# The recurrence's gate products: one 128-row block-diagonal product per gate, or two 64-row tiles of TensorE that each carry both gates of one block

## The chip, the cores and the metric

The kernel runs on one core of a Trainium2 chip. The metric is the device time of one launch in microseconds (us), the median over several runs. One further execution was recorded by the hardware profiler; it gives the rows that are read below.

## The reference, cut to what matters

The model is a two-layer hybrid backbone on 512 latent tokens and 256 context tokens of width 1024. Each layer mixes tokens with four branches (retention, latent attention, a gated linear recurrence called RG-LRU, and a state-space branch), merges them by gates, projects, and then runs a convolutional feed-forward part. The change touches the gates of the recurrence alone. Its 512 channels are 8 blocks of 64; each block has a 64 x 64 weight for each of two gates and two scan directions:

```python
def gates(u, d):
    ub = u.reshape(b, t, LRU_BLOCKS, LRU_BLOCK).astype(f32)
    z = einsum('btnc,gncd->gbtnd', ub, gate_w[d]).reshape(2, b, t, w) + gate_b[d]
    r, i = sigmoid(z[0]), sigmoid(z[1])
    log_a = -LRU_C * r * softplus(-lam[d])
    return exp(log_a), sqrt(-expm1(2.0 * log_a)) * (i * u)
```

The two results feed a scan over the tokens, forward for d = 0 and backward for d = 1.

## The kernel before

Activations lie channel by channel: a feature tile holds 128 channels on the 128 partitions and 768 tokens (256 of context, 512 latent) along the columns. Every float32 product is done as three single-pass products of a value's rounded high part and its low rest (high x high, high x low, low x high), which accumulate in one PSUM bank. A weight unit is a 128 x 1024 array: a DMA on the queue of the sync engine (SP) brings it into a raw buffer (`wr`, 3 buffers), ScalarE (ACT) rounds it into `wh` (L205, 5 buffers), and VectorE (DVE) forms `wl` in two halves (L143, 5 buffers).

The recurrence (`lru`) goes over four feature tiles f, and for each of them over the two directions d. `project(f)` makes the convolved input `u` and an output gate; `scan(f, d)` makes the gates and runs the scan. A feature tile holds two blocks of 64 channels, and the host lays their 64 x 64 weights into a 128 x 128 matrix whose other two quarters are zero; one weight unit holds eight such matrices (two feature tiles, two directions, two gates). In `scan`, for each gate and each of the two token segments (256 and 512 columns), one bank `z` of the four-bank pool `c` takes three products with K = 128 rows and 128 output columns of the array, and one ACT instruction (L1057, tanh with the gate's bias from `gb`) writes it to SBUF. `gb` is half of the gate's bias, by channel, made once a layer in `layer_prep`.

A scheduler sets each engine's order from priorities and dependences. Between the pieces of `lru` it places the work of the queued merges (`merge`: the sigmoid gate and the branch's projection of the branch that was finished before, products into the four banks of pool `g`, read by ACT at L1325), and parts of the modulation weights for later (`ada_all`, L317: four products of 32 output columns side by side on TensorE). After `lru`, the merge of its own results follows, and then the output projection.

Of the kernel before, what the change touches and what calls it, by code (L numbers as in the profile page):

```python
# [8 lines left out]
F32 = mybir.dt.float32  # L9
# [7 lines left out]
P = 128  # L17
# [17 lines left out]
# buffers: 256-column and 512-column scratch, raw weights, their low and high parts, split columns  # L35
MEM = (4, 4, 3, 5, 5, 4)
N_T, N_O, N_WR, N_WL, N_WH, N_V = MEM
# slots of 768 columns in the token mixer; in the feed-forward, and of 512 columns
N_SLOT = 27
# weight of the queued merge work placed behind each piece of a branch  # L40
# [11 lines left out]
# up-projections of latent tokens begun before the last pair of the post norm, by layer  # L52
N_EARLY = (6, 6)
# units of the output projection that go unsplit, in float32 products, for a layer and a token pair
PLAIN = {(0, 0): (0, 1, 2, 3, 4, 5, 6, 7), (1, 2): (3, 5, 7)}
# last units of a product held back so that the output banks finish one after another: output projection, down-projection, its last pair; by layer
STAG = ((0, 2), (0, 0), (3, 5))
# both tiles of a pair normalised before either is scaled, by the same places
PW = ((1, 1), (0, 0), (1, 1))
# order of the pieces of retention: c, d: the two parts of a head; q, k, v, g: projections; y: merges  # L60
RORD = [('c', 0), ('q',), ('d', 0), ('g', 2), ('c', 1), ('k',), ('d', 1), ('v',), ('c', 2), ('g', 3), ('d', 2), ('c', 3), ('y',), ('d', 3), ('y',)]
# query tiles by which transposes and values trail the attention weights; heads by which the sums within chunks trail their matrices
# [5 lines left out]
# buffers that modulation weights take: raw, high, low  # L68
ADA_R = 'hlhl'
ADA_T = ("rhlr", "hlrh", "lrhl", "hlhl")  # L70
# first token pairs loaded behind the first two blocks of modulation weights
FP = {0: (1, 2), 1: (0,)}
# priorities: transposes behind post norms, weights, post norms, split columns, merges
# [6 lines left out]
# offsets of the shape-only tables in the constant array  # L80
# [8 lines left out]
# offsets of the per-partition vectors of a layer  # L89
# [9 lines left out]
def trunk(tc, xin, cc, const, pv, pr, rows, ada_b, ada_w, w_in, w_uq, w_ukv, w_lg, w_br, w_out, w_up, w_dn, out):  # L99
# [9 lines left out]
    with ExitStack() as ctx:  # L109
# [64 lines left out]
        def load_tables(names):  # L174
            """tables that a layer needs for a while."""
# [48 lines left out]
        def fm(wh, wl, nk, x, segs):  # L224
            """feature-major product: weights [128, nk, 128] against x[k] = (hi, lo) over token segments."""
            res = []
            for off, n in segs:
                ps = G()
                for k in range(nk):
                    xh, xl = x[k]  # L230
                    mm3(ps[:, 0:n], wh[:, k, :], wl[:, k, :], xh[:, off:off + n], xl[:, off:off + n], k == 0, k == nk - 1)
                res.append((ps, off, n))
            return res

        def tm(units, cols, x, pairs, begun=None, nk_all=None):
            """token-major product: units = list of ((hi, lo), nk), x[k] = (hi, lo); one bank per token pair; begun: (banks, k) of its first part."""
# [19 lines left out]
        def log1p_of(o, u, n):  # L256
            """o = log1p(u) for u in [0, 1], as 2 atanh(u / (2 + u))."""
# [25 lines left out]
        def ada_part(l, b, tags):  # L283
            """512 columns of a layer's modulation of both streams, four parts over the contraction side by side on TensorE."""
# [10 lines left out]
        def ada_col(l, b, src, n):  # L295
            """bias and place of a vector's blocks b to b + n, by columns: src [128, s, 4 n]"""
# [4 lines left out]
        def ada_store(l, b, r):  # L301
            """the parts' sums"""
# [5 lines left out]
        def ada_all(groups):  # L308
            """four blocks side by side on TensorE."""
# [35 lines left out]
        def ln_stats(halves, eps=LN_EPS):  # L345
            """mean and 1/std of a token tile given as column pieces."""
# [10 lines left out]
        def to_hT(l, which, pair, xh, hT, kps=(0, 1, 2, 3)):  # L357
            """transpose normalised token tiles of a pair, modulate, split."""
# [33 lines left out]
        def load_gate(l, which, s):  # L392
            """a stream's gate spread over the partitions."""
# [6 lines left out]
        def load_bc(l, which):  # L400
            """the norm's weight and bias spread over the partitions, and the latent gate."""
# [8 lines left out]
        def load_res(pair, res):  # L410
            """the residual of a pair of token tiles."""
# [7 lines left out]
        def post_norm(pair, ps, rs, bc, dst, again, wait=False):  # L419
            """new residuals of a token pair from its products ps[a][half]; normalised once more for the next product."""  # L420
# [41 lines left out]
        def pair_of(t, p, spare=False):  # L462
            """the split columns of a pair of token tiles; spare: into the space of a layer's normalised input."""
# [15 lines left out]
        def tm_wide(units, nk, xsl, last=0):  # L479
            """one pair of token tiles against [128, 1024] units, contraction outermost but for the last units."""  # L480
# [37 lines left out]
        # =====================================================================  # L518
        def layer_prep(l):
# [11 lines left out]
            # log(sigmoid(decay)) and softplus(-lambda)  # L531
# [16 lines left out]
            gb = lp.tile([P, 16], F32, tag="gb", name=nm("gb"))  # L548
            ts(gb, V("lgb"), 0.5, MUL)
            q["gb"] = gb  # L550
            q["lg"] = lg
            # halved coefficients
# [12 lines left out]
            # ssd  # L565
# [9 lines left out]
        def retention(q, W, hT, full, outs, begun=None):  # L575
# [6 lines left out]
            def project(dst, h, pairs, begun=None):  # L582
                """a quantity of heads h and h + 1, token-major."""
# [11 lines left out]
            def rope(x3):  # L595
                """on the latent tokens"""
# [9 lines left out]
            def queries(h):  # L606
                """of heads h and h + 1, feature-major; the halves that the rotation mixes are brought together by DMA"""
# [20 lines left out]
            def core(h):  # L628
# [4 lines left out]
                # transposes  # L633
# [15 lines left out]
                # states  # L649
# [18 lines left out]
                # within chunks and outputs  # L668
# [69 lines left out]
            # retention decays  # L738
# [963 lines left out]
```

## Time and profile before

| | us |
|---|---|
| median of 3 runs | 2877.71 |
| lowest and highest run | 2874.56, 2879.39 |
| profiled execution, first to last instruction (span) | 2876.2 |
| TensorE (PE) busy in it | 2824.4 |
| ScalarE (ACT) busy | 1244.0 |
| VectorE (DVE) busy | 1861.2 |

The profiled execution lists no time around its span, and the span lies inside the range of the runs. A matmul's listed duration (0.28 us for 256 columns, 0.39 to 0.40 us for 512) runs from its start to the end of its last result, and the next one starts before that end; what a matmul costs in a full stream is the distance from its start to the next start. `PEld` is the loading of weights into the array, which runs beside the matmuls.

### The profile page before, as it was taken

What the parts mean: (1) busy time and instruction counts of PE and PEld (TensorE: products, weight loads), DVE (VectorE), ACT (ScalarE), POOL (GpSimd) and SP (SyncE); (2) the same over time, 40 slices, a digit from 0 to 9 for tenths busy, and PEclk for the clock granted to TensorE, in tenths of its full rate; (3) what the DMA queues carried; (4) which work ended last, traced back from release to release, by engine and by line L of the source; (5) the groups of instructions that cost most, each with busy time, mean ns of one, the idle gap of its engine ahead of it and who ended that gap; (6) DMA issues with size and microseconds to landing.
All of it is one profiled execution on the core that took longest, in us unless ns stands there. A gap on an engine that the chain in (4) does not pass through costs nothing.

```text
span 2876.2 us, 41735 instructions
## 1 busy us (share of the span) xinstructions
PE 2824.4 (98%) x16136; PEld 2409.4 (84%) x16136; DVE 1861.2 (65%) x3885; ACT 1244.0 (43%) x2190; POOL 53.2 (2%) x70
## 2 busy tenths in 40 slices
PE   7999999999999999999999999999999999899998
PEld 5999878888888886888888779988888888688887
DVE  6463347767566448755557876545887685886667
ACT  4323235434456334533335653244444573453353
POOL 0000000000000001000000000000000000000000
PEclk9999999999999999999999999999999999999999
DMA  7212450445353346422226663122034334543365
GB/s 264 73 42 89 164 176 16 151 165 189 118 169 118 105 153 191 131 61 65 66 88 193 192 196 112 51 90 81 24 103 142 103 118 141 200 148 101 95 197 177
DMA packets 117591, 363.75 MB, mean 126 GB/s; under 512 B 13793, under 2 KB 14177, under 8 KB 117393
## 3 DMA queue, kind: packets, MB, share of 16 engines
q1 hardware_dynamic: 117392, 361.08, 39.0%
q8 instruction: 127, 2.08, 0.3%
q14 instruction: 72, 0.58, 0.1%
HBM read 332.59 MB, written 26.35 MB: 125 GB/s over the span
## 4 chain that ended last, share of the span: by engine, by line
PE 84%; DVE 8%; DMA 4%; ACT 2%; issue 1%; POOL 1%; SPq 0%; POOLq 0%; DVEq 0%; ACTq 0%
PE g L220 18%; PE g L221 17%; PE g L222 17%; PE g L250 4%; PE g L251 4%; PE g L252 4%; PE g L486 3%; PE g L489 3%; PE g L490 2%; DVE wl L143 2%; PE g L946 1%; DVE o L143 1%; DMA wr<-in_w_dn_dram 1%; PE g L317 1%; DVE st L349 1%
## 5 line engine op out<-in xcount | busy, mean ns | idle before, releaser
L143 DVE TENSOR_TENSOR wl<-wr,wh 128x512 fp32r<-128x512 f32 x866 | 566.8, 682 | 459.8 <-ACT wh L205 458.8
L220 PE MATMUL g<-hh,wh 128*128 128x512 f32 (+1 forms) x2384 | 841.8, 353 | 0.8 <-ACT s L510 0.7
L221 PE MATMUL g<-hl,wh 128*128 128x512 f32 (+1 forms) x2384 | 837.7, 351 | 0.0
L222 PE MATMUL g<-hh,wl 128*128 128x512 f32 (+1 forms) x2384 | 837.5, 351 | 0.0
L205 ACT CAST wh<-wr 128x1024 fp32r<-128x1024 f32 (+1 forms) x433 | 451.6, 1045 | 642.8 <-PE g L221 325.1
L220 PEld LDWEIGHTS g<-hh,wh 128*128 128x128 f32 x2384 | 451.1, 189 | 66.5 <-issue 5.9
L222 PEld LDWEIGHTS g<-hh,wl 128*128 128x128 f32 x2384 | 450.8, 189 | 58.3
L221 PEld LDWEIGHTS g<-hl,wh 128*128 128x128 f32 x2384 | 451.2, 189 | 57.1
L251 PE MATMUL g<-wh,hl 128*128 128x256 f32 (+1 forms) x816 | 231.3, 284 | 1.7 <-DVE hl L143 1.7
L250 PE MATMUL g<-wh,hh 128*128 128x256 f32 (+1 forms) x816 | 232.1, 285 | 0.1
L252 PE MATMUL g<-wl,hh 128*128 128x256 f32 (+1 forms) x816 | 231.8, 284 | 0.0
L143 DVE TENSOR_TENSOR s<-s,s 128x256 f32<-128x256 f32 (+4 forms) x332 | 206.7, 645 | 34.7 <-ACT s L1065 14.7
L486 PE MATMUL g<-wh,t 128*128 128x512 f32 x468 | 185.0, 397 | 3.5 <-ACT t L216 2.5
L489 PE MATMUL g<-wh,t 128*128 128x512 f32 x468 | 184.6, 396 | 1.4 <-DVE t L143 1.1
L490 PE MATMUL g<-wl,t 128*128 128x512 f32 x468 | 183.5, 395 | 1.0 <-DVE wl L143 0.6
L221 PE MATMUL g<-s,wh 128*128 128x512 f32 (+1 forms) x452 | 160.6, 355 | 0.0
L220 PE MATMUL g<-s,wh 128*128 128x512 f32 (+1 forms) x452 | 160.2, 354 | 0.0
L222 PE MATMUL g<-s,wl 128*128 128x512 f32 (+1 forms) x452 | 159.9, 354 | 0.0
L251 PEld LDWEIGHTS g<-wh,hl 128*128 128x128 f32 x816 | 156.5, 192 | 2.3 <-DVE hl L143 2.1
L250 PEld LDWEIGHTS g<-wh,hh 128*128 128x128 f32 x816 | 156.7, 192 | 1.5 <-issue 0.8
L252 PEld LDWEIGHTS g<-wl,hh 128*128 128x128 f32 x816 | 156.5, 192 | 0.2
L152 DVE SCALAR_TENSOR_TENSOR s<-g,pv,s 128x511 f32<-128x511 f32 (+2 forms) x176 | 111.7, 643 | 61.2 <-ACT s L510 59.3
(284 smaller groups left out, 4107.3 us busy)
## 6 DMA issues: line engine op xcount, KB each, us to landing
wr<-in_w_in_dram SPq DMA_DIRECT2D x144, 512.0 KB, 3.6
wr<-in_w_dn_dram SPq DMA_DIRECT2D x110, 512.0 KB, 4.4
wr<-in_w_up_dram SPq DMA_DIRECT2D x100, 512.0 KB, 3.7
wh<-in_ada_w_dram SPq DMA_DIRECT2D x46, 512.0 KB, 3.6
wl<-in_ada_w_dram SPq DMA_DIRECT2D x46, 512.0 KB, 4.6
wr<-in_w_out_dram SPq DMA_DIRECT2D x40, 512.0 KB, 4.1
wr<-in_w_br_dram SPq DMA_DIRECT2D x32, 512.0 KB, 3.6
acc<-s SPq DMA_DIRECT2D x24, 384.0 KB, 3.3
```

The lines of the kernel that those rows point to most:

```text
L143: dve.tensor_tensor(out=o, in0=a, in1=b, op=op)
L152: dve.scalar_tensor_tensor(out=o, in0=a, scalar=s, in1=b, op0=op0, op1=op1)
L205: act.copy(hi[:, 0:f], raw[:, 0:f])
L220: pe.matmul(o, lhsT=sh, rhs=mh, start=start, stop=False)
L221: pe.matmul(o, lhsT=sh, rhs=ml, start=False, stop=False)
L222: pe.matmul(o, lhsT=sl, rhs=mh, start=False, stop=stop)
L250: pe.matmul(o, lhsT=sh, rhs=wkh, start=first, stop=False, skip_group_check=True)
L251: pe.matmul(o, lhsT=sl, rhs=wkh, start=False, stop=False, skip_group_check=True)
L252: pe.matmul(o, lhsT=sh, rhs=wkl, start=False, stop=last, skip_group_check=True)
L486: pe.matmul(ps[a][h], lhsT=xh, rhs=wh[:, cs], start=k == 0, stop=wl is None and k == nk - 1)
L489: pe.matmul(ps[a][h], lhsT=xl, rhs=wh[:, cs], start=False, stop=False)
L490: pe.matmul(ps[a][h], lhsT=xh, rhs=wl[:, cs], start=False, stop=k == nk - 1)
```

## The change

Three things change, all for the gates of the recurrence.

1. The weights. Of each 128 x 128 block-diagonal matrix only the two 64 x 64 quarters that aren't zero are fetched (`blocks`): two DMAs of 64 partitions, each with eight pieces of 64 values (256 bytes) a partition, pack them into 512 columns of the raw buffer. Rounding and low part are made of 512 columns in one ACT and one DVE instruction.
2. The products. For a direction, the two gates' 64 columns of one block now stand beside each other, so 64 rows x 128 columns hold both gates of one block. A product of block 0 uses rows 0 to 63 of TensorE and writes bank `z[0]`; the product of block 1 uses rows 64 to 127 and writes `z[1]`. For each segment these come in pairs, for the three parts of the split. Products in all: 12 a scan as before, each with half the rows.
3. The evictions. A bank now holds gate 0 in its upper and gate 1 in its lower 64 partitions, of one block of channels. Each needs its own target, so a bank is read by two ACT instructions on 64 partitions each: 8 a scan, where there were 4. Where source and target lie in different halves, the bias must too: `gb` gets 16 more columns with the halves exchanged, by two DMAs of 64 x 16 values and one more DVE instruction a layer.

The diff's core (the rest removes comments):

```diff
-            gb = lp.tile([P, 16], F32, tag="gb", name=nm("gb"))
-            ts(gb, V("lgb"), 0.5, MUL)
+            gb = lp.tile([P, 32], F32, tag="gb", name=nm("gb"))
+            o = _PO["lgb"][0]
+            for a, b in ((0, 64), (64, 0)):
+                sy.dma_start(out=gb[a:a + 64, 16:32], in_=pv[l][b:b + 64, o:o + 16])
+            ts(gb[:, 0:16], V("lgb"), 0.5, MUL)
+            ts(gb[:, 16:32], gb[:, 16:32], 0.5, MUL)
...
+            def blocks(ap):
+                with tc.high_priority(offset=O_UNIT):
+                    raw, hi, lo = W4("wr", N_WR, F32), W4("wh", N_WH), W4("wl", N_WL)
+                    src = ap.rearrange("p (m b c) -> p m b c", m=8, b=2)
+                    for b in range(2):
+                        r = slice(64 * b, 64 * b + 64)
+                        sy.dma_start(out=raw[r, 0:512].rearrange("p (m c) -> p m c", m=8), in_=src[r, :, b, :])
+                    split(raw[:, 0:512], hi[:, 0:512], lo[:, 0:512])
+                return hi, lo
...
-                        gm[0] = unit(WG(f // 2), shape=(8, 128))
+                        gm[0] = blocks(WG(f // 2))
...
-                for g, dst in ((0, t0), (1, t1)):
-                    i = 4 * (f % 2) + 2 * d + g
-                    j = 8 * d + 4 * g + f
-                    for off, n in (SEG_C, SEG_L):
-                        z = C()
-                        mm3(z[:, 0:n], gm[0][0][:, i, :], gm[0][1][:, i, :], gm[1][0][:, off:off + n], gm[1][1][:, off:off + n], True, True)
-                        act.activation(out=dst[:, off:off + n], in_=z[:, 0:n], func=AF.Tanh, scale=0.5, bias=q["gb"][:, j:j + 1])
+                i = 4 * (f % 2) + 2 * d
+                for off, n in (SEG_C, SEG_L):
+                    z = [C(), C()]
+                    for p, (w, x) in enumerate(((0, 0), (0, 1), (1, 0))):
+                        for b in range(2):
+                            r = slice(64 * b, 64 * b + 64)
+                            pe.matmul(z[b][:, 0:n], lhsT=gm[0][w][r, 64 * i:64 * i + 128], rhs=gm[1][x][r, off:off + n], start=p == 0, stop=p == 2)
+                    for b in range(2):
+                        for g, dst in ((0, t0), (1, t1)):
+                            j = 8 * d + 4 * g + f + (0 if g == b else 16)
+                            r = slice(64 * g, 64 * g + 64)
+                            act.activation(out=dst[64 * b:64 * b + 64, off:off + n], in_=z[b][r, 0:n], func=AF.Tanh, scale=0.5, bias=q["gb"][r, j:j + 1])
```

How the order moves, first on TensorE, at the products of layer 0's first scan (f = 0, d = 0) behind their first part; `c_` are the banks, `s_7966` and `s_7967` the high and low part of `u`, `wh_` and `wl_` the gate weights. Before:

```order
L222 MATMUL g_8010<-hh_104,wl_8007 128x512
L221 MATMUL c_7973<-s_7967,wh_7961 128x256
L222 MATMUL c_7973<-s_7966,wl_7963 128x256
L221 MATMUL c_7978<-s_7967,wh_7961 128x512
L222 MATMUL c_7978<-s_7966,wl_7963 128x512
L221 MATMUL c_7983<-s_7967,wh_7961 128x256
L222 MATMUL c_7983<-s_7966,wl_7963 128x256
L221 MATMUL c_7988<-s_7967,wh_7961 128x512
L222 MATMUL c_7988<-s_7966,wl_7963 128x512
L220 MATMUL g_8010<-hh_106,wh_8005 128x512
```

The same place now, with `s_7969` and `s_7970` for the two parts of `u`:

```order
L222 MATMUL g_8017<-hh_104,wl_8014 128x512
L1074 MATMUL c_7976<-s_7970,wh_7963 128x256
L1074 MATMUL c_7977<-s_7970,wh_7963 128x256
L1074 MATMUL c_7976<-s_7969,wl_7964 128x256
L1074 MATMUL c_7977<-s_7969,wl_7964 128x256
L1074 MATMUL c_7988<-s_7970,wh_7963 128x512
L1074 MATMUL c_7989<-s_7970,wh_7963 128x512
L1074 MATMUL c_7988<-s_7969,wl_7964 128x512
L1074 MATMUL c_7989<-s_7969,wl_7964 128x512
L220 MATMUL g_8017<-hh_106,wh_8012 128x512
```

The products stand in the same place among the merge's (`g_`), and the same number of them; two that follow each other now go to different banks, and belong to different halves of the array's rows. Over the whole program the 192 products stand in 24 unbroken runs among other products: runs of 4 and 8 in a scan of d = 0, and of 12 in one of d = 1.

Second on ACT, the evictions of the same scan and what follows them. Before:

```order
L1057 ACTIVATE s_7970<-c_7973,gb_579 128x256
L1057 ACTIVATE s_7970<-c_7978,gb_579 128x512
L1057 ACTIVATE s_7971<-c_7983,gb_579 128x256
L1057 ACTIVATE s_7971<-c_7988,gb_579 128x512
L1060 ACTIVATE s_7972<-s_7970,l_576 128x768
```

Now:

```order
L1079 ACTIVATE s_7973<-c_7976,gb_579 64x256
L1079 ACTIVATE s_7974<-c_7976,gb_579 64x256
L1079 ACTIVATE s_7973<-c_7977,gb_579 64x256
L1079 ACTIVATE s_7974<-c_7977,gb_579 64x256
L1079 ACTIVATE s_7973<-c_7988,gb_579 64x512
L1079 ACTIVATE s_7974<-c_7988,gb_579 64x512
L1079 ACTIVATE s_7973<-c_7989,gb_579 64x512
L1079 ACTIVATE s_7974<-c_7989,gb_579 64x512
L1082 ACTIVATE s_7975<-s_7973,l_576 128x768
```

Eight instructions on 64 partitions stand where four on 128 stood, ahead of the same chain of exponential and square root.

Third on SP's queue, at the start of the program, where `pv` and `pr` are layer 0's small vectors and the `wr_` are the first weight units of retention. Before:

```order
L522 DMA pv_539<-in_pv_dram 128x277
L524 DMA pr_541<-in_pr_dram 128x48
L198 DMA wr_697<-in_w_in_dram 128x1024
L198 DMA wr_763<-in_w_in_dram 128x1024
L333 DMA o_3782<-in_ada_b_dram 32x512
```

Now:

```order
L522 DMA pv_539<-in_pv_dram 128x277
L524 DMA pr_541<-in_pr_dram 128x48
L552 DMA gb_579<-in_pv_dram 64x16 x2
L198 DMA wr_700<-in_w_in_dram 128x1024
L198 DMA wr_766<-in_w_in_dram 128x1024
```

The two small DMAs of `gb` stand ahead of two weight units; on ACT, DVE and TensorE the work of the next 20 us is then ordered a little differently. Outside of this place, of the two recurrences and of what is woven with them, the engines' orders are as they were, but for layer 1's two `gb` DMAs and its DVE instruction, which now stand behind layer 0's recurrence.

## Rows read from the trace of the kernel before

**Rows 1.** The page's head, and its first part: busy us, share of span, instructions.
```profile
span 2876.2 us, 41735 instructions
PE 2824.4 (98%) x16136; PEld 2409.4 (84%) x16136; DVE 1861.2 (65%) x3885; ACT 1244.0 (43%) x2190; POOL 53.2 (2%) x70
```

**Rows 2.** Both recurrences by stretch: window, length, busy PE, PEld, DVE, ACT, POOL, clock.
```profile
775.00:945.00 170.00, 169.95 (x985) 143.00 (x984) 116.01 (x154) 104.31 (x135) 0.00 (x0) 1.00 0.41 137
...
2195.00:2385.00 190.00, 190.00 (x923) 159.67 (x922) 139.77 (x209) 120.85 (x164) 1.01 (x1) 1.00 0.41 130
```

**Rows 3.** The chain that ended last, within 775 to 945 us: shares by line.
```profile
by line: PE g L220 28.2%; PE g L221 28.1%; PE g L222 28.0%; PE g L317 4.4%; PE c L220 4.0%; PE c L222 3.5%; PE c L221 3.4%; PE c L326 0.5%; issue 0.0%
```

**Rows 4.** Line L222's third products: ns min/median/max, first and last start, forms.
```profile
L222 PE MATMUL c<-s,wl x64: 274/337/497, 779.5 to 2369.6; 128*128 128x256 f32 x32, 128*128 128x512 f32 x32
```

**Rows 5.** PE in order of time, one whole scan (start us, us, operation).
```profile
2264.44 0.28 PE L220 MATMUL c<-s,wh 128*128 128x256 f32 x1
2264.55 0.28 PE L221 MATMUL c<-s,wh 128*128 128x256 f32 x1
...
2266.31 0.39 PE L222 MATMUL c<-s,wl 128*128 128x512 f32 x1
2266.54 0.39 PE L220 MATMUL g<-hh,wh 128*128 128x512 f32 x1
```

**Rows 6.** PE in order of time, round 16 side-by-side products of 32 columns.
```profile
790.52 0.40 PE L221 MATMUL c<-s,wh 128*128 128x512 f32 x1
790.84 0.62 PE L317 MATMUL g<-wh,silu 128*32 128x512 f32 x1
...
791.30 0.59 PE L317 MATMUL g<-wh,silu 128*32 128x512 f32 x1
...
792.16 0.59 PE L317 MATMUL g<-wh,silu 128*32 128x512 f32 x1
...
792.70 0.50 PE L222 MATMUL c<-s,wl 128*128 128x512 f32 x1
793.03 0.28 PE L220 MATMUL c<-s,wh 128*128 128x256 f32 x1
```

**Rows 7.** Weight loads (PEld) in order of time at the same place.
```profile
790.84 0.11 PEld L317 LDWEIGHTS g<-wh,silu 128*32 128x32 f32 x1 [0.36 <-issue]
...
790.89 0.11 PEld L317 LDWEIGHTS g<-wl,silu 128*32 128x32 f32 x1
```

**Rows 8.** PE in order of time: products of 64 columns, each with a 128-column load.
```profile
2117.87 1.00 PE L1244 MATMUL c<-s,s 128*128 128x64 f32 x8
2118.68 0.36 PE L221 MATMUL g<-hl,wh 128*128 128x256 f32 x1
```

**Rows 9.** Groups of ACT instructions by form (count, busy us, mean ns).
```profile
L1057 ACT ACTIVATE s<-c,gb 128x512 f32<-128x512 f32 x32 | 22.2, 693 | 1.0 <-PE c L222 1.0
L1057 ACT ACTIVATE s<-c,gb 128x256 f32<-128x256 f32 x32 | 15.1, 473 | 5.5 <-PE c L222 5.5
L1136 ACT COPY s<-c 16x384 f32<-16x384 f32 x4 | 1.6, 457 | 0.0
```

**Rows 10.** ACT in order of time: a first scan's evictions.
```profile
2258.92 2.10 ACT L1057 ACTIVATE s<-c,gb 128x256 f32<-128x256 f32 x4 [0.82 <-PE c L222]
```

**Rows 11.** DMA issues by line: engine, count, KB each, median us to landing.
```profile
wr<-in_w_lg_dram SPq DMA_DIRECT2D x4, 512.0 KB, 4.3
```

**Rows 12.** SP's queue in order of time: second gate unit of layer 0.
```profile
832.11 0.57 SPq L198 DMA_DIRECT2D wr<-in_w_lg_dram  x1
```

**Rows 13.** PE in order of time: first products with that unit.
```profile
863.50 0.97 PE L220 MATMUL c<-s,wh 128*128 128x256 f32 x4
```

**Rows 14.** DVE in order of time, at the first use of the small vectors.
```profile
37.40 0.17 DVE L534 COPY z<-pv 128x8 f32<-128x8 f32 x1 [0.38 <-DMA pv<-in_pv_dram]
...
45.48 0.17 DVE L147 TENSOR_SCALAR s<-z 128x16 f32<-128x16 f32 x1
```

**Rows 15.** SP's queue in order of time: weight units issued behind the small vectors.
```profile
29.55 11.73 SPq L198 DMA_DIRECT2D wr<-in_w_in_dram  x2
```

## The prediction

> **What bounds the kernel now.** I read the page's first part first, since the share of each engine says where to look: TensorE is busy for 2824.4 of 2876.2 us [rows 1], so what isn't on TensorE hardly shows in the total. Shares are means, so the second view is the busy time of the two stretches that hold the recurrences: PE 169.95 of 170.00 us and 190.00 of 190.00, ACT 104 and 121, DVE 116 and 140, at the granted clock's higher level, 2.4 GHz (the 1.00 in the row) [rows 2]. The third is the chain of waits in the first of them: it consists of PE's matmuls, with no share of ACT, DVE or DMA, and the gate products are the lines "PE c" [rows 3]. So a microsecond taken from PE there is a microsecond of the total, as long as ACT and DVE still deliver; and an operation added to ACT costs nothing until it makes PE wait.
>
> **The change part by part.**
>
> The products. The third products of the gates are 64, half of 256 and half of 512 columns [rows 4]; three products a gate and segment make 192. In a stream, a product of 256 columns costs 0.12 us to the next start, one of 512 costs 0.23, and the twelve of a scan together 2266.54 - 2264.44 = 2.10 us [rows 5]. Sixteen scans (4 tiles, 2 directions, 2 layers) make 33.6 us. Now there are 96 pairs, and if the two of a pair run side by side, a pair costs what one costs: 48 x (0.23 + 0.12) = 16.8 us, so 16.8 us go. The trace has no product of 64 rows. The nearest rows are the products of 32 columns, four side by side: sixteen of them, in four groups, pass between 790.84 and 792.70, and a group takes (792.16 - 791.30) / 2 = 0.43 us, for four products at once [rows 6]. So this chip does run tiles of the array at the same time, by columns. The two bounds are 16.8 us saved and 0 saved (the pairs follow each other as before). I take 16.8, by the row of the side-by-side products.
>
> The loads of weights. Each product loads its own 128 columns of weights. Where the stream is short, the load sets the pace: eight products of 64 columns take 2118.68 - 2117.87 = 0.81 us, 0.10 each [rows 8]. A pair needs two loads, 0.20 us if they follow each other: hidden behind a pair of 512 columns (0.23), not behind one of 256 (0.12). With four column tiles the loads don't follow each other: eight of 32 columns begin between 790.84 and 790.89, each 0.11 long [rows 7], though eight quarters of 0.10 would be 0.20 us one behind the other. I take it that loads into different tiles overlap, and keep the other as a rival.
>
> The changes of tiling. Round the side-by-side products the trace shows a price: 790.52 to 790.84 is 0.32 where a product of 512 costs 0.23 (+0.09), the first group 0.46 instead of 0.43 (+0.03), the last 0.54 (+0.11), and the first product behind it 0.33 instead of 0.23 (+0.10) [rows 6]. That is 0.33 us for a way in and out. The order has 24 runs of paired products among products that use the whole array, so 24 x 0.33 = 7.9 us come back. Bounds: nothing, if a switch to half the rows costs less than one to a quarter of the columns; and, if each side waits for the last result (0.40 - 0.23 = 0.17 us beyond a product's place [rows 5, 6]) and then for a load of 0.11 [rows 7], 0.28 a switch, 24 x 0.56 = 13.4 us. I take 7.9. "TensorEngine Tiling (Array Packing)", section "Key Properties", in the Trainium skill, says that a change of the tiling mode drains TensorE, which a change of tile alone does not. The trace agrees in kind, by the 0.33 us; the rule speaks for keeping the paired products in few long runs, and here runs of 4 and 8 stand where one of 12 could.
>
> The evictions. Four instructions on 128 partitions, 0.473 and 0.693 us by form, become eight on 64. By these rows an eviction of 16 partitions and 384 columns takes 0.457 us [rows 9], so time goes by columns and I charge the eight in full: 4.2 us instead of 2.10 [rows 10], 16 x 2.1 = 34 us more on ACT (at least 0, if half the partitions took half the time). What hides it: ACT has 66 of 170 and 69 of 190 us free [rows 2]. Behind the evictions on ACT stand the exponentials of the same scan and a weight unit's rounding; the one who could wait on PE is the next scan's first product, which needs the four banks again. Before, the evictions ended at 2258.92 + 2.10 = 2261.02 [rows 10] and that product began at 2264.44 [rows 5], 3.4 us later. Of that, 2.1 go to the longer evictions and about 1.0 to PE being early (half of 2.10). Some 0.3 us remain for the last bank, and more for the first two, which are read first and which PE needs first. I cost it at 0, with little cover.
>
> The weights' way. A unit of 512 KB takes 4.3 us to land [rows 11]; now it is half as much in 1024 pieces of 256 bytes, of which the trace has no like. The second unit of layer 0 was issued at 832.11 [rows 12] and first used at 863.50 [rows 13], 31 us later, which holds seven landings. Rounding 512 columns instead of 1024 only frees ACT and DVE. Cost 0.
>
> The small vectors. `gb`'s two DMAs stand ahead of two weight units on SP at the start, which were issued from 29.55 on [rows 15], and its DVE instruction stands right behind the one at 45.48; `pv`, issued before them, was there at 37.4 [rows 14], which leaves 8 us for two small transfers. The weight units behind them come some 2.5 us later (two issues at the 1.3 us spacing of that queue, at most), and the scheduler has put other work of TensorE ahead of them. I take 0 and allow 2 us to either side, for this and for the moved rows elsewhere.
>
> Sum: -16.8 + 7.9 = -8.9 us. Against the profiled execution: a span of 2876.2 - 8.9 = 2867.3 us. That span lies 1.5 us below the median of the runs, 2877.7, and inside their range, so the same step from the median gives 2868.8; I say 2869 us.
>
> **The rivals.**
>
> Loads one behind the other. The pairs of 512 columns still save 48 x 0.23 = 11.0 us, those of 256 only 48 x (0.24 - 0.20) = 1.9. With 7.9 back: -5.0, 2872.7 us. For it: the pace of 0.10 us a load [rows 8]. Against it: the loads of four tiles within 0.05 us [rows 7], though those were of 32 columns each. "TensorE: Matmul & The Clock Gate", section "LDWEIGHTS (loading the stationary operand)", in the Trainium skill, says that a load's time goes by its columns alone, 128 of them taking the same for 32 rows as for 128. By that rule a half-height load isn't cheaper, and this rival is what follows if the two also can't overlap; no row of this trace has a load of 64 rows.
>
> No overlap of row tiles, the one on the other side. The tiles of the trace are column tiles, whose results go to different partitions. Row tiles put two results on the same 128 partitions at the same time, in two banks, and read two halves of the partitions; if the array or the banks take them in turn, the pairs cost 33.6 us as before, and the 24 runs add 7.9: 2877.7 + 7.9 = 2885.6 us. It decides as soon as the pairs save less than 7.9 of 33.6 us, about a quarter, or if a way in and out costs over 16.8 / 24 = 0.70 us.
>
> The evictions come into the chain. If the 0.3 us of cover are missing in the second scan of each feature tile, PE waits there for up to 2.1 us, 8 x 2.1 = 16.8 us: 2885.6 again, with the pairs side by side. For it: the cover. Against it: PE waits for the first bank, not for the last, and there is other work that the scheduler has put between.
>
> **How the numbers follow.** Chances: the forecast 0.52, loads in turn 0.20, no overlap 0.20, evictions 0.08. A difference of 0.2%, 5.8 us, is about what a measurement of this kernel can tell from none, so "faster" lies below 2872.0 and "slower" above 2883.5. The forecast's own range is 2862 to 2873 (switches at 3 to 11 us, 2 us for the order); five sixths of it are faster (0.43), the rest no change. Loads in turn lie at the border: 0.07 faster, 0.13 the same. No overlap: 0.16 slower, 0.04 the same; evictions 0.05 slower, the rest the same. In all 0.50 faster, 0.28 the same, 0.22 slower. The range that holds 8 of 10 is 2862 to 2885: it starts at the forecast's lower end, takes in the loads in turn and some of what the evictions can do, and leaves most of the case without overlap out.
>
> **What would show it.** Right: in the changed trace the two products of a pair start within a few hundredths of a us, a pair of 512 columns comes every 0.23 us and one of 256 every 0.12; the gate products' runs of 12 take about 1.05 us and some 0.3 more at their ends, where a whole scan took 2.10; PE stays busy without a wait in both recurrences, and each of these ends 4 us earlier against its start. Loads in turn show as pairs of 256 columns 0.20 us apart; no overlap as starts 0.12 and 0.23 us apart inside the pairs; the evictions as PE idle before a second scan's first product with ACT named. The forecast is wrong in size if the ways in and out cost much more or less than 0.33 us, and altogether if the products of half the rows start one behind the other.

## The result, and the profile after

The changed kernel takes 2905.9 us, median of its runs, against 2877.0 us of the kernel before beside it: ratio 1.0101, 95% interval 1.0090 to 1.0113. Forecast were 2869 us and a range of 2862 to 2885. It is slower by 29 us, so with the 8.9 us that were to be saved 38 us are missing against the forecast. The profiled execution is the fastest of its four (2899.9 to 2912.9 us), so its trace shows some 22 of the 29 us.

First the page's head and first part, where [rows 1] stood before:

```profile
span 2898.1 us, 41837 instructions
PE 2821.2 (97%) x16136; PEld 2395.3 (83%) x16136; DVE 1858.2 (64%) x3883; ACT 1283.5 (44%) x2254; POOL 53.4 (2%) x70
```

PE is busy for 3.2 us less than before, and the span is 21.9 us longer: what came is time in which PE stands still. ACT has 64 instructions and 39.5 us more. The place is found by cutting the span at the same products of both programs: from the first gate product of a layer to the first product of the output projection (L486) behind it. Columns are those of [rows 2]. Before, layers 0 and 1:

```profile
777.46:1052.35 274.89, 274.85 (x1598) 236.54 (x1599) 153.77 (x210) 125.24 (x166) 0.00 (x0) 1.00 0.38 127
2256.97:2443.30 186.33, 186.33 (x877) 155.65 (x877) 130.44 (x183) 113.23 (x145) 0.00 (x0) 1.00 0.38 123
```

And after:

```profile
780.24:1063.37 283.13, 273.81 (x1598) 229.96 (x1599) 152.53 (x210) 145.40 (x198) 0.00 (x0) 0.99 0.37 122
2265.60:2467.20 201.60, 186.06 (x877) 148.18 (x877) 130.24 (x182) 133.51 (x177) 0.00 (x0) 0.98 0.35 113
```

The counts of products are the same (1598 and 877), so the work is the same. The two stretches became 8.2 and 15.3 us longer, 23.5 us, as much as the two spans differ by. In them PE stands still for 9.3 + 15.5 = 24.9 us, where it stood for none before, and ACT has 40.4 us more. The list of waits names who PE waits for (us in total, times, longest):

```profile
PE g L220 <- ACT s L1347: 14.9, 5, 3.9
PE g L317 <- ACT s L1347: 6.3, 4, 3.1
PE g L220 <- ACT s L216: 2.0, 1, 2.0
PE g L220 <- ACT s L1041: 1.8, 1, 1.8
PE c L1074 <- DVE s L143: 1.2, 3, 0.7
```

L1347 is the merge's tanh (L1325 before), which evicts a bank "g"; L1074 are the gate products. Of the 21.2 us for the tanh, 19.7 lie in the two stretches and 1.4 at 702 us, ahead of them. The waits stand at the *merge's* products and at those of the modulation (L317), which need a bank "g" again, and hardly at a gate product. Who holds the tanh up is seen on ACT in order of time, first scan of layer 1 (where [rows 10] stood):

```profile
2267.58 4.75 ACT L1079 ACTIVATE s<-c,gb 64x256 f32<-64x256 f32 x8 [0.89 <-PE c L1074]
2272.36 1.03 ACT L1082 ACTIVATE s<-s,l 128x768 f32<-128x768 f32 x1
2273.29 1.03 ACT L205 CAST wh<-wr 128x1024 fp32r<-128x1024 f32 x1
2274.23 1.03 ACT L1083 ACTIVATE s<-s,l 128x768 f32<-128x768 f32 x1
2275.28 1.28 ACT L1087 ACT_TABLE_LOAD   x1
2276.57 0.85 ACT L1087 ACTIVATE s<-s 128x768 f32<-128x768 f32 x1
2277.44 1.28 ACT L1347 ACT_TABLE_LOAD   x1
2278.73 0.60 ACT L1347 ACTIVATE s<-g 128x512 f32<-128x512 f32 x1
2279.22 0.94 ACT L1079 ACTIVATE s<-c,gb 64x256 f32<-64x256 f32 x2
```

From 2267.58 to 2279.22 ACT has no gap. One scan is a block of 11 us in order: eight evictions, two functions of the first gate, a weight unit's rounding, the square root between two loads of a function table, and only then the merge's tanh; behind it the next block starts at once. Behind the first block nobody waits. At the end of the second PE is seen waiting, for the tanh of the first row:

```profile
2292.95 0.60 ACT L1347 ACTIVATE s<-g 128x512 f32<-128x512 f32 x1
2290.39 0.39 PE L222 MATMUL g<-hh,wl 128*128 128x512 f32 x1
2293.60 0.50 PE L220 MATMUL g<-hh,wh 128*128 128x512 f32 x1 [2.82 <-ACT s L1347]
```

The pairs did what was forecast. A run of twelve of layer 0, where [rows 6] stood, and its end:

```profile
792.37 0.51 PE L1074 MATMUL c<-s,wh 64*128 64x256 f32 x4
792.72 0.28 PE L1074 MATMUL c<-s,wl 64*128 64x256 f32 x2
792.83 0.64 PE L1074 MATMUL c<-s,wh 64*128 64x512 f32 x4
793.30 0.39 PE L1074 MATMUL c<-s,wl 64*128 64x512 f32 x2
794.63 0.62 PE L317 MATMUL g<-wh,silu 128*32 128x512 f32 x1 [0.93 <-ACT s L1347]
```

It is six pairs (x4 are two pairs, and the two of a pair begin within 0.01 us of each other): 792.72 - 792.37 = 0.35 for two pairs of 256 with the way in, 0.11 for the third, 793.30 - 792.83 = 0.47 for two pairs of 512. A pair costs what one product costs.

### The profile page after: what moved, and what is told of

It reads as the page before. It is cut to its first block, busy times and chain, and to the rows that moved or that the text cites. A ratio compares the mean times of both kernels' runs of the same rounds, so it can differ in the third digit from the quotient of the medians.

```text
span 2898.1 us, 41837 instructions
## 1 busy us (share of the span) xinstructions
PE 2821.2 (97%) x16136; PEld 2395.3 (83%) x16136; DVE 1858.2 (64%) x3883; ACT 1283.5 (44%) x2254; POOL 53.4 (2%) x70
## 4 chain that ended last, share of the span: by engine, by line
PE 80%; DVE 8%; ACT 5%; DMA 4%; issue 2%; POOL 1%; SPq 0%; POOLq 0%; DVEq 0%; ACTq 0%
PE g L220 16%; PE g L221 16%; PE g L222 16%; PE g L251 4%; PE g L252 4%; PE g L250 4%; PE g L486 3%; PE g L489 2%; PE g L490 2%; DVE wl L143 2%; PE g L951 1%; ACT s L1079 1%; DVE o L143 1%; PE g L317 1%; DMA wr<-in_w_dn_dram 1%
## 5 line engine op out<-in xcount | busy, mean ns | idle before, releaser
L222 PE MATMUL g<-hh,wl 128*128 128x512 f32 (+1 forms) x2384 | 839.5, 352 | 0.0
L222 PEld LDWEIGHTS g<-hh,wl 128*128 128x128 f32 x2384 | 451.6, 189 | 59.1 <-issue 0.5
L143 DVE TENSOR_TENSOR s<-s,s 128x256 f32<-128x256 f32 (+4 forms) x332 | 206.9, 644 | 38.8 <-ACT s L596 13.4
L486 PE MATMUL g<-wh,t 128*128 128x512 f32 x468 | 183.8, 395 | 2.3 <-ACT t L216 1.5
L152 DVE SCALAR_TENSOR_TENSOR s<-s,s 128x512 f32<-128x512 f32 (+2 forms) x130 | 98.1, 755 | 97.6 <-ACT s L1079 58.7
L222 PE MATMUL g<-s,wl 128*128 128x512 f32 (+1 forms) x452 | 160.2, 354 | 0.0
```

What stands on the lines that cost most here:

```text
L143: dve.tensor_tensor(out=o, in0=a, in1=b, op=op)
L152: dve.scalar_tensor_tensor(out=o, in0=a, scalar=s, in1=b, op0=op0, op1=op1)
L222: pe.matmul(o, lhsT=sl, rhs=mh, start=False, stop=stop)
L486: pe.matmul(ps[a][h], lhsT=xh, rhs=wh[:, cs], start=k == 0, stop=wl is None and k == nk - 1)
```

## The experiments

All are compared with runs of the kernel before on the same chip. Theory 1: the doubled evictions hold ACT up, and PE waits for the merge's banks. Its rivals: the pairs or changes of tiling (2), the packed weights (3), the small vectors at the start (4).

**Whole banks.** The changed kernel's pairs, with four evictions of 128 partitions.

```diff
-                    for b in range(2):
-                        for g, dst in ((0, t0), (1, t1)):
...
-                            act.activation(out=dst[64 * b:64 * b + 64, off:off + n], in_=z[b][r, 0:n], ...)
+                    for b, dst in ((0, t0), (1, t1)):
+                        j = 8 * d + 4 * b + f
+                        act.activation(out=dst[:, off:off + n], in_=z[b][:, 0:n], ...)
```

> The paired products of the changed kernel as they are, but each of the four banks of a scan is evicted by one instruction on 128 partitions, as before the change, instead of two on 64 (the channels of the two gates come out mixed, so the values aren't the reference's). Theory 1 (the eight evictions hold ScalarE up, and TensorE waits for the merge's banks behind them): the 37.7 us that the forecast missed go, except for 2.8 us at the start, so 2877.0 - 16.8 + 7.9 + 2.8 = 2871 us, 2866 to 2877, and the waits of PE for the line of the merge's tanh are gone from both recurrences. Theory 2 (the pairs themselves or the changes of tiling cost more than the trace of PE shows): it stays at 2895 to 2906. Theory 3 (the packed weights or their place on SP): it stays at 2900 to 2906.

Measured: 2872.6 us, ratio 0.9976 (0.9967 to 0.9986), 6.9 us faster than before. The two stretches, the evictions of layer 1's first scan, and all that is left of waits for the merge's tanh (here L1345; it lies at 701 us, ahead of the stretches):

```profile
779.65:1051.29 271.64, 271.60 (x1599) 229.13 (x1599) 152.57 (x210) 124.87 (x166) 0.00 (x0) 1.00 0.39 127
2253.80:2436.20 182.40, 182.40 (x876) 147.29 (x876) 129.60 (x182) 112.09 (x144) 0.00 (x0) 1.00 0.40 124
```

```profile
2255.78 1.99 ACT L1077 ACTIVATE s<-c,gb 128x256 f32<-128x256 f32 x4 [0.89 <-PE c L1074]
```

```profile
PE g L317 <- ACT s L1345: 0.9, 1, 0.9
```

PE has no gap in either stretch, and they are 3.3 and 3.9 us shorter than before. So the pairs and the changes of tiling together give 7.2 us back: theory 2 falls. Against the changed kernel the stretches are 484.7 - 454.0 = 30.7 us shorter: 24.9 of them PE's idle time, the rest longer products (459.9 us busy against 454.0). Those are seen behind the waits: in the changed kernel's stretch from 2405 us on, at the end of a wait of 3.87 us, the granted clock is 0.50, its lower level of 1.2 GHz, and rises back in the next 5 us:

```profile
2405.00:2410.00 5.00, 2.95 (x6) 1.90 (x7) 4.48 (x6) 1.11 (x2) 0.00 (x0) 0.50 0.61 212
2410.00:2415.00 5.00, 5.00 (x20) 4.05 (x20) 1.80 (x3) 0.41 (x1) 0.00 (x0) 0.87 0.31 105
```

There are three such places in the two stretches, each at the end of a wait (from 834, 937 and 2404 us on), 13.4 us in all with PE busy for 10.9 of them. At half the clock, half of that is lost, 5.4 us: an estimate that covers most of the 5.9. With whole banks the clock is 1.00 in both stretches.

**The kernel before with halved evictions.** The reverse: only the evictions doubled.

```diff
-                        act.activation(out=dst[:, off:off + n], in_=z[:, 0:n], ..., bias=q["gb"][:, j:j + 1])
+                        for r in (slice(0, 64), slice(64, 128)):
+                            act.activation(out=dst[r, off:off + n], in_=z[r, 0:n], ..., bias=q["gb"][r, j:j + 1])
```

> The kernel before, its 192 whole products, weights and small vectors untouched, but each bank of a scan is evicted by two instructions on 64 partitions each. Theory 1: ScalarE has 16 x 2.66 = 42.6 us more, PE waits for the merge's banks as in the changed kernel, though it comes to each scan's end about 1 us later, so somewhat less than the 37.7 us missed: +20 us, 2890 to 2910. Theories 2 and 3: 2877, plus or minus 3. A side question: the eight evictions of the changed kernel began 0.49 and 0.71 us apart, with no overlap, the four of the kernel before 0.35 to 0.59; if 64 partitions are the reason, it is so here too, and if it is the moving from one half of the partitions to the other (half of the changed kernel's do), then pairs here begin closer together.

Measured: 2903.6 us, ratio 1.0089 (1.0073 to 1.0104), +25 us. The same waits, without a paired product in the program, and the same block on ACT (the merge's tanh is L1326 here):

```profile
PE g L220 <- ACT s L1326: 12.6, 5, 2.9
PE g L317 <- ACT s L1326: 2.5, 2, 1.7
```

```profile
2275.31 4.74 ACT L1058 ACTIVATE s<-c,gb 64x256 f32<-64x256 f32 x8 [0.81 <-PE c L222]
```

The eight take 4.74 us though each writes the partitions that it reads. So the moving between halves isn't the reason for the lack of overlap. Nor is a shared bank: in the changed kernel's block at 2267.58 two evictions of one bank begin 0.48 or 0.70 us apart, and it is 0.50 or 0.71 where the next one reads another bank. Nor is it few partitions by themselves: the four copies from 16 partitions in [rows 9], of 457 ns each, are busy for 1.6 us together, not 1.83. What the evictions without overlap share is that each reads another half of the partitions than the one before. One place of this run fits that: there an eviction from partitions 0 to 63 is followed by an instruction on 128 partitions, which begins 0.1 us before it ends:

```profile
2392.01 0.47 ACT L1058 ACTIVATE s<-c,gb 64x256 f32<-64x256 f32 x1 [1.59 <-PE c L222]
2392.38 0.62 ACT L1040 ACTIVATE s<-s 128x512 f32<-128x512 f32 x1
```

Behind an eviction from partitions 64 to 127, an instruction on 128 never does so (17 times). No run takes the evictions half by half, so this is a reading and not shown.

**Whole weight units.**

```diff
-                        gm[0] = blocks(WG(f // 2))
+                        gm[0] = unit(WG(f // 2), shape=(8, 128))
...
-                            pe.matmul(z[b][:, 0:n], lhsT=gm[0][w][r, 64 * i:64 * i + 128], rhs=gm[1][x][r, off:off + n], start=p == 0, stop=p == 2)
+                            pe.matmul(z[b][:, 0:n], lhsT=gm[0][w][r, i, :], rhs=gm[1][x][r, off:off + n], start=p == 0, stop=p == 2)
```

> The changed kernel with the gate weights loaded and rounded as whole units of 1024 columns, by the two-queue path of all other units, as before the change; the paired products read the first 64 rows and the last 64 of a product's 128 columns (other values than the reference's, the same sizes). Theory 3 (the transfer in pieces of 256 bytes, or its place on SP, delays the recurrence): back to 2870 to 2880. Theories 1 and 2: 2906, plus or minus 4.

Measured: 2913.4 us, ratio 1.0113 (1.0100 to 1.0126). The median lies 3 us above the range of theories 1 and 2; by the ratio it is within noise of the changed kernel (1.0101, 1.0090 to 1.0113). Nothing comes back; theory 3 falls.

**Without the small transfers.**

```diff
-            for a, b in ((0, 64), (64, 0)):
-                sy.dma_start(out=gb[a:a + 64, 16:32], in_=pv[l][b:b + 64, o:o + 16])
-            ts(gb[:, 16:32], gb[:, 16:32], 0.5, MUL)
+            ts(gb[:, 16:32], V("lgb"), 0.5, MUL)
```

> The changed kernel without the two small transfers that bring the halves of the bias vectors crosswise (the second 16 columns of that tile are copied from the first, so half of the biases are another channel's). Theory 4 (the small transfers ahead of two weight units at the start cost the 2.8 us by which the first gate product comes later): 2903, 2900 to 2905, with the first gate product back to 777 to 778 us. Rival: the 2.8 us come from the scheduler's other order and from the granted clock there (0.78 against 0.91 between 20 and 40 us), and it stays at 2906, plus or minus 2. All other theories expect the rest of the span unchanged.

Measured: 2909.0 us, ratio 1.0098 (1.0084 to 1.0113), 1 us above the rival's range, and the first evictions begin at 782.6 us as in the changed kernel (782.7). The 2.8 us at the start aren't these transfers. They needn't be the change at all: two runs that leave the start as it was before, with the same order on PE, ACT and DVE up to there, have their first gate product at 780.50 (halved evictions) and 780.38 us (the control below), where the trace of before has it at 777.46:

```profile
780.50 0.97 PE L220 MATMUL c<-s,wh 128*128 128x256 f32 x4
780.38 0.97 PE L220 MATMUL c<-s,wh 128*128 128x256 f32 x4
```

So executions with the same start differ by 3 us there.

**Without the square root.** This asks whether the evictions as such or ACT's whole block decides: eight evictions stay, 3.4 us of other ACT work per scan goes.

```diff
-                act.activation(out=s, in_=s, func=AF.Sqrt, scale=0.25)
+                ts(s, s, 0.25, MUL)
```

> The changed kernel with its eight evictions, but without the square root of each scan (left out; its factor 0.25 is taken by an instruction on VectorE, so the values aren't the reference's). With it go the two loads of a function table round it: 0.85 + 2 x 1.28 = 3.4 us of ScalarE in each of 16 scans, more than the 2.66 us that the doubled evictions added. Theory 1a (ScalarE's whole work between a merge's products and its eviction decides): PE's waits for the merge's tanh go, 2866 to 2878 us. Theory 1b (the block of eight evictions alone holds the merge's eviction up, whatever follows it): the waits stay, 2895 to 2906.

Measured: 2876.8 us, ratio 0.9989 (0.9980 to 0.9997): against the changed kernel 1.12%, some 32 us, are gone, with the evictions as long as ever. Of the 19.7 us of waits for the merge's tanh in the two stretches 0.6 are left (second fence), and 5.5 of all 24.9:

```profile
2265.23 4.72 ACT L1079 ACTIVATE s<-c,gb 64x256 f32<-64x256 f32 x8
```

```profile
PE g L220 <- ACT s L1347: 0.6, 1, 0.6
```

The control, the same edit in the kernel before:

> The control of the run without the square root: the kernel before with the same instruction left out (other values than the reference's; the factor 0.25 by VectorE). If ScalarE only matters where it makes PE wait (theory 1a), then nothing is to be had here, since PE waits for it 1.3 us in both recurrences: 2876 to 2880, ratio 0.999 to 1.001. If a shorter scan helps by itself, 2865 to 2872, and the recovery in the changed kernel would say little on the evictions.

Measured: 2879.1 us, ratio 0.9999 (0.9990 to 1.0008). (The 1.3 us named above are waits of the output projection, behind the recurrences; inside of them PE waits for nothing.) The same 3.4 us of ACT a scan are worth some 32 us in the one kernel and nothing in the other. ACT's sum in a block decides, and it does so only past a point; how far the kernel before stood from it is worked out below.

**Four tiles of 64 x 64, and unsplit products.** Two tries for a better kernel, in float32 products (one instead of three). In the first the second gate's halves come out crosswise, and two transfers exchange them.

```diff
-                            pe.matmul(z[b][:, 0:n], lhsT=gm[0][w][r, 64 * i:64 * i + 128], rhs=gm[1][x][r, off:off + n], start=p == 0, stop=p == 2)
+                            pe.matmul(z[g][o:o + 64, 0:n], lhsT=gm[0][r, 64 * (i + g):64 * (i + g) + 64], rhs=u[r, off:off + n], start=True, stop=True)
...
+                for b in range(2):
+                    pool.dma_start(out=t1[64 * b:64 * b + 64, :], in_=x1[64 - 64 * b:128 - 64 * b, :])
```

> Another way to use half the array: both gates of both blocks of 64 channels as four tiles of 64 rows and 64 columns, in whole float32 products (one instead of three, no rounding of weights and u). The first gate's bank holds its channels in order; the second gate's two blocks stand crosswise, so that each bank is still evicted by one instruction on 128 partitions, and two transfers on GpSimd's queue put the second gate's halves in their place. A float32 product of 512 columns comes every 0.43 us in the trace of before (line of the output projection's unsplit units), one of 256 I put at half. If the four tiles run side by side, a scan takes 0.65 us instead of 2.10, 16 ways in and out cost 0.33: 2877 - 23.2 + 5.3 = 2859 us, 2854 to 2866. If only two of the four run together: 2877 - 12.8 + 5.3 = 2870. One after the other: 2.6 us a scan, 2890. Theory 1 says that the evictions cost nothing here; if the transfers delay the scans, PE waits elsewhere and the gain shrinks.

> The same, with the two transfers on SP's queue, where weight units wait behind a transfer whose data isn't ready. If that queue has room: the same time as with GpSimd's queue, 2859. If it hasn't: some 5 to 15 us longer, with PE or ScalarE waiting for weight units in the recurrences.

The second is the kernel before with `pe.matmul(z[:, 0:n], lhsT=gm[0][:, i, :], rhs=u[:, off:off + n], start=True, stop=True)` in place of the three products.

> The kernel before with its gate products as whole float32 products on the full array (one instead of three, no rounding of weights and u), no tiling, four evictions on 128 partitions. By 0.43 us for 512 columns and half of it for 256, a scan takes 2 x 0.65 = 1.30 us instead of 2.10: 2877 - 16 x 0.8 = 2864 us, 2860 to 2868. ScalarE and VectorE lose the rounding of u and of four weight units, which shouldn't show. Theory 1 expects no new wait, since ScalarE has less to do, not more.

Measured: 2880.5 us (ratio 1.0004, 0.9994 to 1.0014), 2877.1 (0.9994, 0.9985 to 1.0003) and 2885.2 (1.0017, 1.0008 to 1.0026), all slower than forecast. My price was half of the true one: the trace holds two records for a float32 product, so 0.43 us is half a product. In the last kernel one scan's 4 products are 8 records (2270.91 to 2273.08 is 2.17 us at the starts of the first and of the product behind them):

```profile
2270.91 2.74 PE L1055 MATMUL c<-s,wr 128*128 128x256 f32 x8
2273.08 0.79 PE L220 MATMUL g<-hh,wh 128*128 128x512 f32 x1
```

That product behind them needs 0.63 us to its next start where one costs 0.23, so a scan takes some 2.6 us against 2.10. The four tiles ran at the same time: 16 records, 2263.06 to 2264.51, are 1.45 us a scan. That is 0.65 less than 2.10, and 0.46 less with 0.19 for the way in and out (by the starts round it). So 16 x 0.46 = 7.4 us should be won; with GpSimd's queue it was 1.2 us slower, with SP's 1.7 faster, both within noise of the kernel before. About half of what is missing is a wait at the gate products for u (4.8 us with GpSimd's queue, 3.0 with SP's); the other half stays open. The product row is that of SP's queue, the wait that of GpSimd's:

```profile
2263.06 1.52 PE L1071 MATMUL c<-s,wr 64*64 64x256 f32 x16
2264.51 0.50 PE L220 MATMUL g<-hh,wh 128*128 128x512 f32 x1
```

```profile
PE c L1071 <- DVE s L152: 4.8, 2, 4.1
```

**Pairs with whole banks, made complete.** Each bank goes with one eviction to a tile of its own; then the halves are sorted. First by four transfers, in the second and third with the second block's weight columns exchanged, so that only the second gate needs transfers. The code is the second's:

```diff
+                    for b, dst in ((0, x0), (1, x1)):
+                        act.activation(out=dst[:, off:off + n], in_=z[b][:, 0:n], func=AF.Tanh, scale=0.5, bias=q["gz"][:, j:j + 1])
...
+                dve.tensor_copy(t0[lo_h, :], x0[lo_h, :])
+                dve.tensor_copy(t0[hi_h, :], x1[hi_h, :])
+                sy.dma_start(out=t1[lo_h, :], in_=x0[hi_h, :])
+                sy.dma_start(out=t1[hi_h, :], in_=x1[lo_h, :])
```

> The changed kernel's paired products with four evictions of whole banks, made complete: each bank holds both gates of one block, is evicted with one instruction into a tile of its own, and four transfers from SBUF to SBUF sort the halves into the two gates' tiles. Theory 1: as with the evictions alone, 2872 us (ratio 0.9976), if the transfers are hidden. Against it: the exponentials now wait for a transfer of some 2 to 4 us, and they stand in order on ScalarE before the merge's tanh; then 2880 to 2895.

Measured: 2921.8 us, ratio 1.0154 (1.0140 to 1.0168), above both forecasts and the slowest of all, with four whole evictions a scan. ACT's exponential waits for the transfers (group by line, the last part is the idle time before it and who ended it), and PE behind it:

```profile
L1090 ACT ACTIVATE s<-s,l 128x768 f32<-128x768 f32 x16 | 16.5, 1030 | 42.2 <-DMA s<-s 39.7 <-issue 2.4
```

```profile
PE g L220 <- ACT s L1355: 18.0, 5, 4.8
PE g L317 <- ACT s L1355: 10.5, 4, 3.8
```

Against the whole banks alone, 42.2 us of standing still in ACT's block cost 1.8%, 51 us; the 16 x 2.65 = 42.4 us of longer evictions cost 1.25%, 36 us. So a wait in the block cost about as much as work. Not all of it need be that wait: SP's queue, which also issues weight units, stood still for 74 us at these transfers until ACT had made what they move, and what that cost isn't separated.

> The same with the columns of the second block's weights exchanged, so that the first gate's halves stand at their own partitions in the two tiles: two copies of 64 x 768 on VectorE bring the first gate together, two transfers the second, which is needed late. If VectorE has room: 2872 us, 2868 to 2876. VectorE gets 16 x 2 copies, at most 0.95 us each by its other instructions of 768 columns, 30 us in all, in stretches where it is busy for 16 of 20 us: if that makes PE wait, 2880 or more.

Measured: 2873.6 us, ratio 0.9988 (0.9979 to 0.9997). It leaves nothing out and is faster than the kernel before by 3.5 us (0.9 to 6.0). The price of the sorting on DVE and the wait that is left on ACT:

```profile
L1087 DVE COPY s<-s 64x768 f32<-64x768 f32 x16 | 8.9, 558 | 0.5
L1086 DVE COPY s<-s 64x768 f32<-64x768 f32 x16 | 8.8, 549 | 12.6 <-ACT s L1084 12.6
```

```profile
L1092 ACT ACTIVATE s<-s,l 128x768 f32<-128x768 f32 x16 | 16.6, 1035 | 6.5 <-DVE s L1087 6.5
```

> The same with the two copies on GpSimd, which has nothing else to do there. If a copy takes 1 to 2 us, the exponentials wait about that long more than with VectorE, VectorE is as free as before, and the time is 2872 us, 2868 to 2878; if GpSimd is much slower, ScalarE waits at the exponentials and PE behind it, 2880 to 2900.

Measured: 2874.5 us, ratio 0.9987 (0.9978 to 0.9996), the same with a copy at 0.82 to 0.99 us.

## Why the prediction was wrong, point by point

**The products: right.** A pair starts with both products at once, and 256 and 512 columns come every 0.11 to 0.12 and 0.23 us. **The loads: right**, they overlap; the pace of the pairs shows it. **The changes of tiling: right in size.** The two stretches fell by 7.2 us with whole banks, forecast were 8.9, with a way in and out at 0.33 us (7.2 makes it 0.40). One row was misread on the way: a float32 product leaves two records, as a run above shows, so the sixteen rows of [rows 6] are eight products, and a group of four records at 0.43 us is half of four products. That four tiles run at once stands all the same. "Loads one behind the other" (5.0) and the forecast are within the interval of the whole time (4.0 to 9.5), but the starts in the pairs decide for the forecast; "no overlap" is out.

**The evictions: the step that failed.** The prediction said: "the one who could wait on PE is the next scan's first product, which needs the four banks again", and "I cost it at 0, with little cover." The charge was near (4.2 us forecast for eight, 4.75 measured), and the free share of ACT was read rightly. Wrong was who waits. I looked for the reader of the evicted banks "c"; PE waited for another pool of banks, "g", whose tanh stands behind the evictions in ACT's order. So the cover of 0.3 us was worked out for the wrong wait, and the price was capped at 16.8 us for a second scan's first product, where 24.9 us of waits (19.7 of them for the tanh) and 5.9 of longer products came. The rival "evictions come into the chain" had the right engine, the wrong place and a chance of 0.08.

The free share [rows 2] couldn't show it: 66 of 170 and 69 of 190 us are means, and much of that free time lies elsewhere than in a scan's block. Of the first, 24 us are weight roundings that wait until PE gives a buffer back, and of the second 28 (the first two lines, and the third):

```profile
ACT wh L205 <- PE g L221: 15.0, 6, 4.9
ACT wh L205 <- PE g L317: 8.7, 3, 3.7
ACT wh L205 <- PE g L221: 27.9, 15, 4.7
```

The question is how long ACT works from the evictions to the operation that frees the bank that PE runs out of, and how many products PE has in hand for so long. In layer 1 that operation is the tanh behind the second scan of a feature tile; all four tiles show the wait there, and the first is worked out here. Before, the tanh ended at 2279.19 + 0.60 = 2279.79, which is 20.9 us after the first scan's first eviction (2258.92 [rows 10]), and the product that needs the bank began at 2283.04, 3.2 us later:

```profile
2279.19 0.60 ACT L1325 ACTIVATE s<-g 128x512 f32<-128x512 f32 x1
2283.04 0.39 PE L220 MATMUL g<-hh,wh 128*128 128x512 f32 x1
```

After, it ended at 2292.95 + 0.60 = 2293.55, which is 26.0 us after 2267.58: 5.1 longer, for two scans with 2.65 more each. PE had its products before that one (the same number of them) done at 2290.39 + 0.23 = 2290.62, 23.0 us after 2267.58 instead of 24.1, since the pairs had made it 1.1 us earlier. Of a cover of 3.2 us, 5.1 and 1.1 are taken: PE should stand still for some 3.0 us, and 2.82 were seen. So this was the cover to work out, over two scans and for bank "g", and not the 0.3 us.

The Trainium skill has a rule that speaks of it: "TensorEngine Tiling (Array Packing)", section "PSUM Bottleneck", says that tiling speeds up TensorE but not the emptying of PSUM, which may then become the limit. The trace agrees and goes further: here the emptying didn't only stay, it doubled (4.75 against 2.10 us), since the tiles' results lie crosswise to the tiles that they go to.

**The weights' way: right**, 0 (whole units change nothing). **The small vectors: right**, 0. The first gate product came 2.8 us later, outside the 2 us allowed, but executions of an unchanged start differ by as much. **The chances** add up to 0.29 for the same and 0.21 for slower, not 0.28 and 0.22; nothing hangs on it.

## What to carry to other kernels

Don't price an operation that is added to a half-idle engine by the engine's free share. Follow the order on that engine from the added operation to the one that frees what the bound engine runs out of (here two blocks on), add up what lies between, a wait in it as well as work, and compare with what the bound engine has in hand; the buffer that runs out need not be one that the change touches. A layout that halves the products but makes results cross partitions moves its cost to the evictions: keep evictions whole, and sort on an engine that has room.

## What the runs showed of the hardware

- An eviction from 64 partitions costs ACT what one from 128 does: 683 and 468 ns by form against 693 and 473 [rows 9]. Eight that take the halves in turn don't overlap, 4.75 us against 2.10 for four whole ones [rows 10]; copies from 16 partitions do [rows 9].
- Two products of 64 rows run at the same time at full pace, into two banks of the same 128 partitions; four of 64 x 64 do too (1.45 us for a scan's 16 records).
- A float32 product leaves two records in the trace, each of 0.43 us for 512 columns: 0.86 us, more than three rounded ones at 0.23.
- A transfer of 192 KB from SBUF to SBUF that an engine waits for in order is dear: 2.5 us a scan for the exponential (39.7 us over 16 scans).
